# The sample's cached attention in a hybrid encoder step: one group of tokens, or shared between two

## The chip, the core and the metric

The kernel runs on one core of one Trainium2 chip. Its time is the device time of one execution in microseconds (us). A core has five engines, each with an in-order queue: TensorE (PE; its weight loads are listed as PEld), VectorE (DVE), ScalarE (ACT), GpSimd (POOL) and SyncE (SP), which here only issues DMA transfers. Matrix products land in eight PSUM banks of 128 x 512 fp32 numbers; everything else lies in SBUF or in main memory.

## The reference

One layer with two branches of 8 heads of 128 channels each, over 1024 new frames of a prompt (eight tiles of 128 rows) and 8 x 16 frames of running streams (one tile, the sample), with cached keys and values of 1024 past frames for each stream:

```python
h = rms_norm(x, norm_pre)                       # x: (rows, 2048)
p = h @ w_in                                    # 8 column blocks of 1024:
q_sb, k_sb, v_sb, gate_sb, q_r, k_r, v_r, gate_r = split(p)
# stick-breaking branch, strictly causal; of the sample over cache and new keys
z = q_sb @ k_sb.T * 128 ** -0.5
log_keep = where(strict, log_sigmoid(-z), 0)
a = where(strict, exp(log_sigmoid(z) + later(log_keep)), 0)
o_sb = a @ v_sb
# retention branch: rope on q_r, k_r, decay masks, running state in and out
y = concat(head_rms_norm(o_sb) * silu(gate_sb), head_rms_norm(o_r) * silu(gate_r))
x + rms_norm(y @ w_out, norm_post)
```

The new keys, values and states are outputs too.

## The kernel before

The rows are worked in two groups: the first is tiles 0 to 3 and the sample (640 columns of the transposed activations, in pieces of 256 and 384), the second tiles 4 to 7 (512 columns, one piece). Each group runs through the eight heads. For a head, `project` makes the columns 4, 5 and 7 of the input projection (retention's query, key, gate), then 0, 1 and 3 (the stick-breaking query, key, gate); `project_rows` makes the value rows of both heads of a pair at the even head. Weights and activations are split in a high and a low part, and each product is made of three (`products`, line 206, 48 steps for a projection). This is most of PE's work; its weights come through SP's queue in small loads (L192, L237) that ACT and DVE split (L127, L128).

Everything else is done by jobs: generators that are advanced by `tick()`, one job at most for each step of `products`, and that say after how many ticks they want the next turn. The constants `D_...` hold these waits; where one is a pair, the first is for the first group. They decide where in PE's program a job's matmuls stand. The engines' queues are then filled by a list scheduler when the kernel is built, and the hardware runs each queue in order.

For each head there is a job for retention (`ret_branch`), one for the prompt's attention (`sb_branch`, with `stick_breaking`: scores z at L535, the value product at L559), and in the first group one for the sample (`decode`), which lasts about one head's period:

- Keys: sixteen chunks of cached keys, each by four DMAs of POOL's queue (L585, buffer kc), are transposed by DVE (L610, kcT). After four chunks, four matmuls of 32 rows, one for each column tile, make a quarter of the scores (zc, L601); two quarters share one PSUM bank of the pool psz, which has three. ACT takes two sigmoids of each half (kp at L459, be at L460). The scores against the new keys (zn, L626) go into another bank of psz.
- Weights: `weights` masks on POOL, then DVE scans (L476) and multiplies (L477). `turn_out` writes the result to a scratch tile s_bd through ACT's queue, `turn_in` reads it back in four pieces through SP's (L441), and DVE transposes it into kp (L635).
- Values: the new values (L641), then eight sets of four 32-row matmuls over the cached values (L648, buffer vc), accumulate in a bank of psa, the pool with one bank that the prompt's and retention's products use too. The cached values come in eight loads of 512 KB through SP's queue (L616). They share five buffers (`V_BUFS`) with kcT; five loads are put in the queue at once, ahead of the scores' end.

The normalisation and gate of the sample's result are done with the prompt's, in one `Out` of five tiles. Beside it, the sample's retention state is worked in `retention` (pSs, L739), in both versions in the first group.

Between the groups `load_moving` brings the second group's activations (s_h, staged in the first 50 us) through four buffers mr of SBUF and splits them, tied to the last gate's and the next query's projection; the same function brings the gated results s_y to the output projection. The first output panel (`panel0`, L889 to L891) is made beside the last jobs.

## Time and profile before

| | before |
|---|---|
| time, median of 3 runs | 2466.65 us |
| lowest and highest | 2466.45, 2468.67 us |
| profiled execution: span | 2465.5 us |
| matmuls on PE | 14832 |
| moved by DMA | 418.65 MB, mean 170 GB/s |

The span lies 1.15 us under the median; what the time has beyond the span lies around the first and last instruction. From the trace's timeline the execution has these stages, in us from the span's start: normalising and staging the rows, 0 to 50; the first group, to 1172; the second, to 2027; the last jobs beside the first output panel, to 2082; the output projection, to 2465. In the views, a matmul's row gives its line, its tiles (out<-in), its shape, and how many equal ones follow each other; "idle before" is what the engine waited just ahead of it, and for whom.

### The profile page before, as it was taken

To read this page: it belongs to the slowest core of one execution; us is meant where nothing else is said; L and a number is where in the kernel's file an instruction comes from. 1 tells how busy PE (TensorE), PEld (TensorE's weight loads), DVE (VectorE), ACT (ScalarE), POOL (GpSimd) and SP (SyncE) were. 2 spreads that over 40 slices of the span, in tenths; PEclk is the share of its full clock that TensorE was granted. 3 is DMA by queue.
4 is the path that set the end of the run, shared out by engine and by line. 5 is a ranking of instruction groups with operands and counts; after the bars stand their busy time and mean duration, and the time that the engine had idled before them with its cause. 6 is when DMAs were issued, how large, how long until landed. Compare 5 with 4: busy or idle time off the path is not lost.

```text
span 2465.5 us, 40324 instructions
## 1 busy us (share of the span) xinstructions
PE 2368.1 (96%) x14832; PEld 2098.0 (85%) x14832; DVE 1250.1 (51%) x2362; ACT 904.3 (37%) x1913; POOL 643.7 (26%) x1029
## 2 busy tenths in 40 slices
PE   7999899989999999999899999999999998999998
PEld 7999889879898888989588898888889877778787
DVE  8245454444444454445545554554564565564544
ACT  6323232323223232323334434344344343543343
POOL 3244353433344344333402111120220211000000
PEclk9999999999999999999899999999999999999999
DMA  7769788785958768598955665565664566765554
GB/s 242 167 151 208 145 199 165 173 171 138 210 134 202 160 155 189 134 217 177 219 153 149 155 152 145 143 164 134 154 158 128 153 151 179 242 215 163 184 182 135
DMA packets 673094, 418.65 MB, mean 170 GB/s; under 512 B 223744, under 2 KB 617984, under 8 KB 670464
## 3 DMA queue, kind: packets, MB, share of 16 engines
q1 hardware_dynamic: 523760, 285.99, 46.3%
q0 software_dynamic: 32256, 71.36, 12.9%
q10 hardware_dynamic: 116880, 58.74, 8.5%
q8 instruction: 116, 1.90, 0.3%
q14 instruction: 82, 0.67, 0.1%
HBM read 336.24 MB, written 79.69 MB: 169 GB/s over the span
## 4 chain that ended last, share of the span: by engine, by line
PE 72%; DMA 12%; issue 8%; DVE 5%; ACT 1%; POOL 1%; SPq 1%; DVEq 0%; ACTq 0%; POOLq 0%
PE acc L206 37%; PE accn L252 14%; PE a L890 4%; PE a L891 4%; PE a L889 4%; PE pa L559 2%; DMA vc<-cache_sb_v 2%; PE z L535 1%; DMA s_be<-kb 1%; DMA wr<-w_in 1%; DMA mr<-s_y 1%; PE zc L601 1%; DMA kb<-s_be 1%; DMA kc<-cache_sb_k 1%; DMA ro<-s_rk 1%
## 5 line engine op out<-in xcount | busy, mean ns | idle before, releaser
L206 PE MATMUL acc<-mh,wh 128*128 128x256 f32 (+2 forms) x2304 | 670.8, 341 | 6.8 <-ACT rv L262 4.3
L206 PE MATMUL acc<-ml,wh 128*128 128x256 f32 (+2 forms) x2304 | 676.5, 343 | 0.0
L206 PE MATMUL acc<-mh,wl 128*128 128x256 f32 (+2 forms) x2304 | 670.3, 341 | 6.1 <-DVE wl L128 6.1
L128 DVE TENSOR_TENSOR wl<-wr,wh 128x512 fp32r<-128x512 f32 (+1 forms) x576 | 395.2, 690 | 531.9 <-ACT wh L127 522.0
L127 ACT ACTIVATE wh<-wr 128x512 fp32r<-128x512 f32 (+1 forms) x576 | 357.6, 625 | 756.6 <-PE acc L206 366.5
L206 PEld LDWEIGHTS acc<-mh,wh 128*128 128x128 f32 x2304 | 425.6, 189 | 51.5 <-issue 14.5
L206 PEld LDWEIGHTS acc<-mh,wl 128*128 128x128 f32 x2304 | 425.0, 189 | 50.4 <-issue 12.4
L206 PEld LDWEIGHTS acc<-ml,wh 128*128 128x128 f32 x2304 | 422.5, 189 | 39.5 <-issue 12.4
L585 POOL DMA_DIRECT2D kc<-cache_sb_k x512 | 331.4, 653 | 374.9 <-DVE kcT L610 175.0
L252 PE MATMUL accn<-whn,mh 128*128 128x256 f32 x1152 | 332.8, 290 | 1.1 <-ACT whn L127 1.1
L252 PE MATMUL accn<-wln,mh 128*128 128x256 f32 x1152 | 327.1, 284 | 5.6 <-DVE wln L128 5.6
L252 PE MATMUL accn<-whn,ml 128*128 128x256 f32 x1152 | 326.8, 284 | 0.0
L252 PEld LDWEIGHTS accn<-whn,mh 128*128 128x128 f32 x1152 | 221.5, 192 | 14.6 <-issue 11.0
L252 PEld LDWEIGHTS accn<-wln,mh 128*128 128x128 f32 x1152 | 221.7, 192 | 8.6 <-DVE wln L128 7.2
L890 PE MATMUL a<-wl,mh 128*128 128x512 f32 (+1 forms) x576 | 220.7, 383 | 7.8 <-DVE wl L128 7.7
L252 PEld LDWEIGHTS accn<-whn,ml 128*128 128x128 f32 x1152 | 221.4, 192 | 1.7 <-issue 1.7
L889 PE MATMUL a<-wh,mh 128*128 128x512 f32 (+1 forms) x576 | 219.2, 383 | 3.6 <-ACT wh L127 2.6
L891 PE MATMUL a<-wh,ml 128*128 128x512 f32 (+1 forms) x576 | 220.3, 382 | 0.0
L890 PEld LDWEIGHTS a<-wl,mh 128*128 128x128 f32 x576 | 108.7, 189 | 31.2 <-DVE wl L128 10.6
L127 ACT ACTIVATE whn<-wrn 128x512 fp32r<-128x512 f32 x128 | 79.8, 634 | 151.2 <-PE acc L206 38.3
L889 PEld LDWEIGHTS a<-wh,mh 128*128 128x128 f32 x576 | 109.0, 189 | 26.4 <-ACT wh L127 4.1
L441 POOL DMA_DIRECT2D be<-s_be x128 | 94.0, 741 | 139.8 <-DMA s_be<-be 122.3
(184 smaller groups left out, 2578.8 us busy)
## 6 DMA issues: line engine op xcount, KB each, us to landing
wr<-w_in SPq DMA_DIRECT2D x384, 256.0 KB, 4.0
wr<-w_out SPq DMA_DIRECT2D x184, 256.0 KB, 3.5
wrn<-w_in SPq DMA_DIRECT2D x128, 256.0 KB, 3.3
kc<-cache_sb_k POOLq DMA_DIRECT2D x512, 64.0 KB, 4.5
vc<-cache_sb_v SPq DMA_DIRECT2D x64, 512.0 KB, 8.5
xt<-x_prompt SPq DMA_DIRECT2D x8, 1024.0 KB, 6.5
xr<-x_prompt SPq DMA_DIRECT2D x8, 1024.0 KB, 6.6
out<-out ACTq DMA_DIRECT2D x12, 512.0 KB, 2.9
```

Source lines behind the costliest of these rows:

```text
L127: nc.scalar.activation(hi, src, AF.Copy)
L128: nc.vector.tensor_tensor(lo, src, hi.bitcast(F32), ALU.subtract)
L206: last = nc.tensor.matmul(a[:, :m], lhs[:, j, :], rhs[w][:, j, o : o + m], start=(w == 0 and j == 0 and n == 0), stop=(w == KT // WQ - 1 a ...
L252: nc.tensor.matmul(a, lhs[q][:, jj, ts], rhs[:, j, :], start=(w == 0 and j == 0 and n == 0 and t % 2 == 0), stop=(w == KT // 2 - 1 and j = ...
L441: q.dma_start(raw[32 * i : 32 * i + 32, :].rearrange("p (k a) -> p k a", a=32), s[:, :, 32 * i : 32 * i + 32].rearrange("k (j b) a -> b (k ...
L535: nc.tensor.matmul(z[:, :c], q2[a][:, i * P : (i + 1) * P], k2[b][:, s : s + c], start=(m == 0), stop=(m == 2),)
L559: nc.tensor.matmul(po[:, :P], at[:, j, :], vn[:, j, :], start=(j == 0), stop=(j == t))
L585: nc.gpsimd.dma_start(kc[32 * i : 32 * i + 32, :].rearrange("p (k d) -> p k d", d=32), cache_k[0, 2 * c + j, s * 512 : (s + 1) * 512, h, 3 ...
L601: nc.tensor.matmul(z[r, :], qp[:, j, r], ready[c // 2][:, c % 2, :], start=(j == 0), stop=(j == 1))
L889: nc.tensor.matmul(a[:, :width], hi[q][:, j, ts], wh, start=(k == 0), stop=False)
L890: nc.tensor.matmul(a[:, :width], hi[q][:, j, ts], wl, start=False, stop=False)
L891: nc.tensor.matmul(a[:, :width], lo[q][:, j, ts], wh, start=False, stop=(k == KT - 1))
```

## The change

The sample's stick-breaking heads are shared between the groups: the even heads' query, key and gate are made in the first group, the odd ones' in the second, which takes the heads of a pair in the other order (1, 0, 3, 2, and so on). A group's heads without the sample have 512 columns in one piece, those with it 640 in two. A decode job runs over two head periods, with larger waits, in a bank of its own (psd; psz goes from three banks to two), with an `Out` and an end of its own (`ends`, scratch s_ys). The four score matmuls of a quarter are kept together, tile 3 first. Cached values are loaded one by one, and the buffers shrink: three for kcT and vc, two for kc, two for mr. The scores of five tiles come in 512 + 128 columns (computed as 256) where they were 384 + 256, as old and new keys now lie in two tiles of 512. s_h holds the sample's rows too.

```diff
-D_ZC = 12
-D_ROW = 18
-D_VC = 9
-V_BUFS = 5
+D_ZC = 24
+D_ROW = 24
+D_VC = 20
+D_DTO = 40
+D_DTI = 20
+D_DTR = 6
+V_BUFS = 3
...
+    def takes_sample(gi, h):
+        return h % 2 == gi
...
-            r = wp.tile([P, n], F32, name="mr", tag="mr", bufs=4)
-            nc.sync.dma_start(r, src(k))
+            r = wp.tile([P, n], F32, name="mr", tag="mr", bufs=2)
+            for o, m, ap in src(k):
+                nc.sync.dma_start(r[:, o : o + m], ap)
...
+                    nc.vector.tensor_tensor(
+                        hs[:, WQ * q : WQ * (q + 1), :],
+                        mov[0][q][:, :, NB_TOK:].bitcast(F32),
+                        mov[1][q][:, :, NB_TOK:].bitcast(F32),
+                        ALU.add,
+                    )
...
-        psz = s1.enter_context(tc.tile_pool(name="psz", bufs=3, space=PSUM))
+        psz = s1.enter_context(tc.tile_pool(name="psz", bufs=2, space=PSUM))
         psa = s1.enter_context(tc.tile_pool(name="psa", bufs=1, space=PSUM))
+        psd = s1.enter_context(tc.tile_pool(name="psd", bufs=1, space=PSUM))
...
         def z_pieces(n):
-            if n == 5 * P:
-                return (0, 3 * P), (3 * P, 2 * P)
             return [(s, min(512, n - s)) for s in range(0, n, 512)]
...
-        def decode(h, out, qs, rest):
+        def decode(h, qs, rest):
+            out = Out(1, "os")
...
-                kc = ip.tile([P, 512], F32, name="kc", tag="kc", bufs=3)
+                kc = dp.tile([P, 512], F32, name="kc", tag="kc", bufs=2)
...
-                    for c in range(4):
+                    done = None
+                    for c in (3, 0, 1, 2):
                         r = slice(32 * c, 32 * c + 32)
-                        nc.tensor.matmul(
+                        with tc.issue_after(done.ins) if done else nullcontext():
+                            mm = nc.tensor.matmul(
...
-            values = [load_v(k) for k in range(V_BUFS)]
-            while "kT" not in rest:
+            while "ks" not in rest:
                 yield 3
-            z = psz.tile([P, 512], F32, name="zn", tag="z")
+            z = bank("zn")
...
             turned = turn_out(be.rearrange("p (k c) -> p k c", c=P), f"s_bd{h}")
-            yield D_TO[phase[0]]
+            load_v()
+            yield D_DTO
             turn_in(turned, be, nc.sync)
-            yield D_TI[phase[0]]
+            load_v()
+            yield D_DTI
             nc.vector.transpose(kp[:, :n], be)
-            yield D_TR[phase[0]]
+            load_v()
+            yield D_DTR
...
-            po = acc_tile()
+            po = bank("pd")
...
-                if k + V_BUFS < 8:
-                    values.append(load_v(k + V_BUFS))
+                if len(values) < 8:
+                    load_v()
...
         for gi, g in enumerate(GROUPS):
...
+            for i in range(H):
+                h = i ^ gi
+                sample = takes_sample(gi, h)
+                pieces = WITH_SAMPLE if sample else PROMPT_ONLY
...
-                acc = project(g, mov, col(0, h))
+                acc = project(pieces, mov, col(0, h))
...
+                if sample:
+                    drain(dec_job)
+                    while len(ends) > 1:
+                        drain(ends.pop(0))
...
+                    dec_job = Job(decode(h, qs, rest), D_DEC)
```

How this moves the instructions is seen in the engines' programs, where each row is a line, an operation and its tiles, with a count of equal ones in a row. First PE at the end of a head's cache scores; this is the last head of the first group before:

```order
L601 MATMUL zc<-kcT,qp 32x512 x2
L626 MATMUL zn<-kT,qs 128x128
L559 MATMUL pa<-vn,kb 128x128
L601 MATMUL zc<-kcT,qp 32x512
L535 MATMUL z<-kh,qh 128x512
L535 MATMUL z<-kl,qh 128x512
L535 MATMUL z<-kh,ql 128x512
L206 MATMUL acc_13148<-mh_12926,wh 128x512
L206 MATMUL acc_13148<-ml_12927,wh 128x512
L252 MATMUL accn_13294<-whn,mh_12778 128x256
```

And PE at the last decode that begins in the first group now (L622 is the cache score's line, L650 the new key's, L216 the projection's):

```order
L622 MATMUL zc<-kcT,qp 32x512 x4
L216 MATMUL acc_11342<-mh_159,wh 128x512
L216 MATMUL acc_11342<-ml_160,wh 128x512
L216 MATMUL acc_11342<-mh_159,wl 128x512
L216 MATMUL acc_11342<-mh_159,wh 128x512
L729 MATMUL pS<-rv,rkn 128x128
L216 MATMUL acc_11342<-ml_160,wh 128x512
L650 MATMUL zn<-ks,qs 128x128
L216 MATMUL acc_11342<-mh_159,wl 128x512
```

The set of four stood in three places, with zn ahead of some of them; now it is one piece, and zn follows it.

Second, SP's queue at one head's value loads (L616 before) and the return of the turned weights (be); wr, wrn are weights, st and dT belong to retention:

```order
L616 DMA vc<-cache_sb_v 128x8x128 x4
L192 DMA wr<-w_in 128x4x128 x4
L724 DMA st<-state_ret 128x2x128
L192 DMA wr<-w_in 128x4x128 x2
L616 DMA vc<-cache_sb_v 128x8x128
L192 DMA wr<-w_in 128x4x128
L441 DMA be<-s_bd_5630 32x36x32 x4
L192 DMA wr<-w_in 128x4x128 x4
L616 DMA vc<-cache_sb_v 128x8x128 x3
```

The same queue now (L642 is the value load, L459 the return, L202 the weights):

```order
L642 DMA vc<-cache_sb_v 128x8x128
L459 DMA so<-s_o_2_4_5508 32x16x32 x4
L459 DMA ro<-s_rk_3_5670 32x20x32 x4
L202 DMA wr<-w_in 128x4x128 x8
L642 DMA vc<-cache_sb_v 128x8x128 x2
L202 DMA wr<-w_in 128x4x128 x2
L459 DMA be<-s_bd_5861 32x36x32 x4
L202 DMA wr<-w_in 128x4x128 x4
L691 DMA dT<-c_dt 128x256
```

Of the five value loads ahead of the return three are left; the other five follow one by one behind the value products.

Third, PE beside the first output panel (a), where a decode now has its value products (L667 and L674, bank pd):

```order
L576 MATMUL pa<-vn,kp 128x128 x5
L667 MATMUL pd<-vs,kp 128x128
L674 MATMUL pd<-vc,kp 32x256 x12
L961 MATMUL a_21334<-wh_21675,mh_21301 128x512
L961 MATMUL a_21335<-wh_21675,mh_21301 128x512
L961 MATMUL a_21336<-wh_21675,mh_21301 128x512
L962 MATMUL a_21334<-wl_21676,mh_21301 128x512
L963 MATMUL a_21334<-wh_21675,ml_21302 128x512
L962 MATMUL a_21335<-wl_21676,mh_21301 128x512
L963 MATMUL a_21335<-wh_21675,ml_21302 128x512
L962 MATMUL a_21336<-wl_21676,mh_21301 128x512
L674 MATMUL pd<-vc,kp 32x256 x4
```

Before, only the prompt's value products (pa<-vn,kp) stood among these panel matmuls; now three sets of the decode's stand in one piece behind them, and the fourth eight panel matmuls later.

236 lines of the change are left out of this document (141 added, 95 removed).

## The prediction

> **What bounds the kernel now.** I read the page's busy line first, then its chain that ended last, then the busy time by stage, then PE's waits stage by stage.
>
> ```profile
> PE 2368.1 (96%) x14832; PEld 2098.0 (85%) x14832; DVE 1250.1 (51%) x2362; ACT 904.3 (37%) x1913; POOL 643.7 (26%) x1029
> PE 72%; DMA 12%; issue 8%; DVE 5%; ACT 1%; POOL 1%; SPq 1%; DVEq 0%; ACTq 0%; POOLq 0%
> ...
> 50.00:338.00 288.00, 280.01 (x2038) 262.20 (x2037) 131.17 (x267) 95.06 (x203) 106.97 (x176) 0.99 0.75 166
> 1390.00:1596.00 206.00, 205.73 (x1178) 180.70 (x1177) 109.61 (x192) 82.97 (x171) 36.07 (x56) 1.00 0.59 149
> 2027.00:2082.00 55.00, 44.97 (x203) 36.18 (x202) 33.43 (x50) 22.14 (x47) 15.91 (x23) 0.94 0.80 207
> ```
>
> The first line is the page's, the next the shares of the chain, the rest stretches of the span with the busy time of PE, PEld, DVE, ACT and POOL, the granted clock, the DMA share and GB/s. PE is the bound: 96% busy, 72% of the chain. A pair of heads in the first group, whose work runs from 50 to 1172, takes 288 us and leaves PE idle for 8 of them, with DMA at 0.75. The second group, from 1172 to 2027, has no decode beyond its first 60 us; a pair there takes 206.00 us, of which PE is busy 205.73, with DMA at 0.59. So the decode's waits can only be won in the first group, and the second is a place without slack into which half of the decode moves.
>
> PE's waits (engine, line, released by: us in all, times, longest), four lines of the first group, then two of the stretch from 2027 on:
>
> ```profile
> PE pa L648 <- DMA vc<-cache_sb_v: 9.3, 4, 4.6
> PE pa L641 <- DVE kp L635: 8.0, 2, 7.3
> PE pa L559 <- DVE so L656: 7.5, 3, 4.0
> PE zc L601 <- DVE kcT L610: 3.5, 3, 2.1
> ...
> PE a L890 <- DVE wl L128: 7.7, 5, 3.0
> PE pa L559 <- DVE kp L525: 6.7, 3, 2.9
> ```
>
> The four are all the decode's: its cached values late, its turned weights late, the prompt's value products kept out of the one shared bank until the decode's result is read, its transposed keys late. Together 9.3 + 8.0 + 7.5 + 3.5 = 28.3 us, the most that removing them can save directly.
>
> **The change part by part.** Terms are against the profiled execution, whose span is 2465.5 us; the shown median, 2466.65, lies 1.15 above it, and I add the sum to the median.
>
> (a) **Matmul pieces.** PE pays for each switch to the decode's 32-row matmuls:
>
> ```profile
> 1197.11 1.05 PE L601 MATMUL zc<-kcT,qp 128*32 128x512 f32 x4
> 1198.10 0.49 PE L626 MATMUL zn<-kT,qs 128*128 128x128 f32 x2
> ...
> 1199.52 1.04 PE L601 MATMUL zc<-kcT,qp 128*32 128x512 f32 x2 [0.71 <-DVE kcT L610]
> 1200.50 0.50 PE L535 MATMUL z<-kh,qh 128*128 128x512 f32 x1
> ...
> 661.14 0.64 PE L648 MATMUL pa<-vc,kp 128*32 128x256 f32 x8
> 661.71 0.38 PE L252 MATMUL accn<-whn,ml 128*128 128x256 f32 x1
> ...
> 172.99 0.71 PE L739 MATMUL pSs<-rv,rkn 32*128 32x128 f32 x8
> ...
> L535 PE MATMUL z<-kl,qh 128*128 128x512 f32 x40 | 15.8, 395 | 0.0
> L535 PE MATMUL z<-kl,qh 128*128 128x384 f32 x24 | 8.1, 338 | 0.0
> ```
>
> From a start to the next, a piece of cache scores (zc) takes 0.99 us with 4 records and 0.98 with 2: splitting a set of four column tiles costs the whole piece again. In PE's program the pieces fall from 45 to 32, since the four are now held together: 13 x 0.98, **-13 us**. The pieces of the value product over the cache rise from 55 to 63, at 661.71 - 661.14 = 0.57 us: +4.6. Those of the sample's retention state (pSs) rise from 16 to 23; between nothing and 0.71 each I take 0.3, as most of such a piece is its own work: +2. Of the 384-column scores of the prompt 24 become 512 wide: 24 x (395 - 338) ns = +1.4. Together **+8 us**. All main matmuls keep their counts; the sample columns merely move between the groups.
>
> (b) **The four waits of the first group.** A head has twice the time, the bank is the decode's own, and half the heads are gone. The shared-bank wait (7.5) goes; of the others I leave 4 us: **-24 us** (bounds 0 and -28.3). What is late next there is the turn of (d).
>
> A long wait also costs clock (columns as in the stretches above):
>
> ```profile
> 520.00:525.00 5.00, 0.00 (x0) 0.00 (x0) 0.80 (x2) 1.26 (x2) 0.67 (x2) 0.70 1.23 203
> 525.00:530.00 5.00, 3.68 (x22) 2.22 (x23) 4.44 (x9) 0.97 (x2) 0.00 (x0) 0.50 0.14 24
> 530.00:535.00 5.00, 5.00 (x32) 4.40 (x31) 1.12 (x2) 0.63 (x1) 0.00 (x0) 0.77 0.65 170
> ```
>
> After the 7.3-us wait the clock is 0.50, and 0.77 in the next stretch: with PE busy 3.68 at half rate and 5.00 at 0.77, some 1.8 + 1.2 = 3 us are lost, 0.4 per us waited. For the waits of 7.3, 4.6 and 4.0: **-6 us**. [...]
>
> (c) **The new bank.** Cache scores and new-key scores (zn) now take turns in one bank, so zn waits for the sigmoids of the second half of the cache scores:
>
> ```profile
> L459 ACT ACTIVATE kp<-zc x16: 578/598/602, 167.2 to 1208.6; 128x512 f32<-128x512 f32 x16
> 1405.98 23.83 PE acc L206 x104
> ```
>
> The first row is one of two such sigmoids, together 1.2 us after the scores; the second is a stretch of the chain in the second group, 23.83 / 104 = 0.229 us a main matmul. zn stands about six of those behind the scores, 1.4 us. The cover is just enough if ACT comes at once; behind zn stands the whole projection. I take 8 x 0.4 = 3 us, and 2 for prompt scores with two banks instead of three: **+5 us** (bounds 0, and 20 if ACT, 37% busy, is mostly occupied).
>
> (d) **The turn of the decode's weights** (scan, product, out to memory, back, 32x32 transpose), between zn and the first value product:
>
> ```profile
> 630.02 0.49 PE L626 MATMUL zn<-kT,qs 128*128 128x128 f32 x2
> 636.80 2.56 DVE L476 TENSOR_TENSOR_SCAN kp<-kp 128x1152 f32<-128x1152 f32 x1 [1.04 <-ACT kp L459]
> 639.49 1.36 DVE L477 TENSOR_TENSOR be<-be,kp 128x1152 f32<-128x1152 f32 x1
> 651.20 3.59 SPq L441 DMA_DIRECT2D be<-s_bd  x4
> 659.22 1.38 DVE L635 STREAM_TRANSPOSE kp<-be 128x1152 f32<-128x1152 f32 x1 [5.49 <-DMA be<-s_bd]
> 660.75 0.46 PE L641 MATMUL pa<-vn,kp 128*128 128x128 f32 x2
> ...
> s_bd<-be ACTq DMA_DIRECT2D x8, 576.0 KB, 7.9
> be<-s_bd SPq DMA_DIRECT2D x32, 144.0 KB, 4.8
> ...
> DMA to landing us min/median/max: 2.3/5.1/10.3
> ```
>
> Here the chain took 660.75 - 630.02 = 30.7 us, of which 659.22 - 640.85 = 18.4 was the way through memory and 12.3 the rest. With both ways at 2.3, the shortest landing (the last row is of the scratch tile), and 3.6 for issuing the four returns, the way is 8.2 and the chain 20.5; with the medians, 7.9 and 4.8, it is 28.6. In PE's program of the new kernel 72 main matmuls at 0.229 (16.5 us), 17 of the prompt's scores and five of its value products (4.1) stand between the two in the second group, 20.6 us; in the first about five more, and for the very last decode 58 main matmuls (13.3) and 5.3 of scores, 18.6. In the first group it is covered. In the second the DMA share was 0.59 and rises to about 0.68 with the caches; I take the middle, 24.5: a stall of 3.9 us in three decodes, 11 to 12, and, these being short, 1 to 2 for the clock: **+13 us** (bounds 0 and +45). Behind the waiting product stand all projections.
>
> (e) **From group to group** the moving rows are staged again, now through two buffers instead of four, and 640 wide instead of 512, while a decode runs its value product:
>
> ```profile
> 1210.00:1220.00 10.00, 7.37 (x56) 7.04 (x54) 9.01 (x12) 1.59 (x4) 4.09 (x5) 0.92 1.00 283
> 1220.00:1230.00 10.00, 4.54 (x19) 4.04 (x19) 2.75 (x6) 1.89 (x3) 3.68 (x6) 0.50 0.91 219
> ```
>
> Before, this place already lost 2.6 + 5.5 = 8 us idle and about 2.3 to the clock, with DMA full. The last decode of the first group again stands here, and in PE's program its first twelve value matmuls (three loads) are in one piece; the fourth load can begin only when the first has been used. **+3 us** (bounds -10, all of it gone, and +15).
>
> (f) **The tail.** One decode now ends beside the first output panel, where before there was none:
>
> ```profile
> vc<-cache_sb_v SPq DMA_DIRECT2D x64, 512.0 KB, 8.5
> ```
>
> Again three loads are used in one piece, the fourth lands 8.5 us later, with some 2 us of panel matmuls ahead of it in the queue: 6.5, and the turn has 18.6 of cover for 24.5: 5.9. Part coincides with the 6.7 us that PE waits there for the prompt's turned weights: 12.4 less about half of that, **+9 us** (bounds -3 and +20).
>
> (g) **At no cost:** staging the sample's rows (four more DVE sums and one write, in the start, beside projections); the issues of cached keys, with two buffers for three, since a chunk has at least 24 products x 0.229 = 5.5 us, two 11, for four issues of 0.649, a landing of 4.5 and a transpose; V loads one by one, each behind its buffer in SP's queue, with the weights' loads behind them:
>
> ```profile
> L585 POOL DMA_DIRECT2D kc<-cache_sb_k x512: 649/649/871, 105.4 to 1202.2; - x171
> kc<-cache_sb_k POOLq DMA_DIRECT2D x512, 64.0 KB, 4.5
> ```
>
> If those covers fail, each head pays a wait like the 4.6 above.
>
> **Sum:** -13 + 8 - 24 - 6 + 5 + 13 + 3 + 9 = -5; 2466.65 - 5 = 2461.65, given as **2462 us**.
>
> **The rivals.** A: the turn fits its cover also in the second group and the tail costs little. Then (d) is 0, (e) 0, (c) +3, (f) +3: -13 + 8 - 24 - 6 + 3 + 3 = -29, **2438**. For it speaks the lower DMA share of the second group; against it that even the shortest chain, 20.5, has 0.1 us to spare.
>
> B, on the other side: the chain keeps its 30.7 us in the second group, because DVE's in-order queue and SP's, not DMA, make it. Three decodes stall 30.7 - 20.6 = 10.1 us, 30, and 0.4 x 30 = 12 for the clock: +42 for +13, **2491**. The stall, with its clock, costs 3 x 1.4 us per us of chain; all else makes -18, so it decides against the change from 20.6 + 18 / 4.2, about 25 us, and by a measurable amount from 26. For it speaks the 10.3 us from the product's end, 640.85, to the return's issue, 651.20; against it that this was at DMA 0.74 and over.
>
> C: two staging buffers starve the change of groups; at +18 instead of +3, +15, and the fourth V load at the same place, a little: **2478**.
>
> [...]
>
> **How the numbers follow.** A measurement of this kernel can tell about 0.2%, 4.9 us, so faster is below 2461.7 and slower above 2471.6. The forecast, with its own range 2450 to 2474, has 0.42 (0.20 faster, 0.17 same, 0.05 slower); A 0.26, B 0.23, C 0.07, D 0.02. Faster 0.46, same 0.17, slower 0.37. The range runs from 2430, A with the transition's idle time gone too, to 2490, nearly B: half of B lies beyond it, D, and a little of A.
>
> **What would show it.** In the new profile: zc in pieces of full sets, 32 of them; no wait of the prompt's value product for the decode's result; waits for cached values under 4 us in the first group. The wait of the new-value product (pd from the turned kp) is the decisive line: 0 in the second group for A, about 3 x 4 for the forecast, 3 x 10 at a clock of 0.5 for B. A pair there should take 206 us, plus 4 x 0.98 and 8 x 0.57 for the decode's pieces and, for the sample's columns of one head, a quarter of 144 x 0.229, some 223, plus these stalls; a wait of zn for ACT of over a microsecond would show (c) too small. I am wrong altogether if the second group waits on its weights, since I priced SP's queue at nothing.

## The result

The changed kernel takes 2523.27 us (median of 4, 2519.45 to 2527.46) against 2467.66 us for the kernel before on the same chip: ratio 1.0232, 95% interval 1.0213 to 1.0251. It is slower by 2.3%, some 56 us, where 2462 us and a range up to 2490 were forecast.

The page of the changed kernel, its busy line:

```profile
PE 2388.8 (95%) x14832; PEld 2111.3 (84%) x14832; DVE 1271.1 (50%) x2454; ACT 908.0 (36%) x1939; POOL 643.6 (26%) x1029
```

The span of this execution is 2517.7 us, 52.2 more than before's 2465.5. PE is busy 2388.8 - 2368.1 = 20.7 us longer and idle 31.5 us longer. The longer busy time goes with a lower clock: the matmuls are the same in number, and the mean granted clock is 0.975 where it was 0.987. Where the time is lost is seen when the span is cut at the first projection of the second group and at the first matmul of the output panel. First the kernel before, then the changed one (stretch, its length, busy time of PE, PEld, DVE, ACT, POOL, granted clock, DMA share, GB/s):

```profile
50.00:1172.00 1122.00, 1082.71 (x7871) 996.47 (x7870) 528.93 (x1068) 349.96 (x775) 434.53 (x722) 0.99 0.76 171
1172.00:2022.00 850.00, 836.90 (x4778) 723.55 (x4777) 449.29 (x800) 336.32 (x696) 154.67 (x244) 0.99 0.61 153
2022.00:2465.00 443.00, 414.05 (x1947) 344.45 (x1945) 233.50 (x400) 183.47 (x390) 34.50 (x33) 0.98 0.60 187
```

```profile
50.00:1064.00 1014.00, 992.24 (x6923) 924.35 (x6923) 475.05 (x1003) 337.00 (x737) 282.73 (x481) 0.99 0.65 154
1064.00:2052.00 988.00, 937.63 (x5663) 804.52 (x5662) 520.42 (x944) 354.51 (x754) 306.63 (x484) 0.97 0.74 166
2052.00:2517.00 465.00, 424.32 (x2010) 348.80 (x2009) 237.34 (x411) 182.24 (x395) 34.25 (x35) 0.96 0.61 189
```

Idle time of PE is length less busy. In the first group it falls from 39.3 to 21.8 us (-17.5), in the second it rises from 13.1 to 50.4 (+37.3), from the first panel on from 29.0 to 40.7 (+11.7). The first group ends 108 us earlier, as it should with half the decode gone, and the second lasts 138 us longer.

PE's waits in the changed kernel (engine, line, released by: us in all, times, longest):

```profile
PE z L552 <- ACT be L479: 24.5, 8, 6.7
PE accn L262 <- DVE rk L305: 18.0, 3, 6.5
PE pa L576 <- DVE kp L541: 16.4, 5, 8.3
...
PE pd L674 <- DMA vc<-cache_sb_v: 9.2, 6, 3.2
PE acc L216 <- ACT mh L136: 8.3, 4, 4.2
...
PE zc L622 <- DVE kcT L632: 5.2, 4, 1.3
...
PE pd L667 <- DVE kp L661: 1.8, 2, 1.0
```

The decode's own waits are nearly gone: 1.8 us for its turned weights (before 8.0), none of the prompt's value products for the decode's result (7.5). But the three largest are new or grown, and none of them is the decode's: the prompt's scores wait for a sigmoid, the value rows for the rotary sums of the keys, the prompt's value product for its turned weights.

### The wait for the sigmoid

ACT in the second group, at the end of a decode's scores (start, us, engine, line; ACTq rows are issues of DMA in ACT's queue), then PE and DVE at the same place:

```profile
1321.28 0.62 ACT L478 ACTIVATE kp<-z 128x512 f32<-128x512 f32 x1
1321.64 0.40 ACTq L810 DMA_DIRECT2D out<-kn  x1
1328.38 0.39 ACTq L453 DMA_DIRECT2D s_bd<-be  x1
1331.98 0.32 ACTq L810 DMA_DIRECT2D out<-kn  x1
1332.48 0.60 ACT L479 ACTIVATE be<-z 128x512 f32<-128x512 f32 x1 [10.59 <-DMA vc<-cache_sb_v]
```

```profile
1326.03 0.39 PE L216 MATMUL acc<-mh,wl 128*128 128x512 f32 x1
1333.13 0.80 PE L552 MATMUL z<-kph,qh 128*128 128x512 f32 x1 [6.72 <-ACT be L479]
1333.72 0.63 PE L552 MATMUL z<-kpl,qh 128*128 128x512 f32 x1
```

```profile
1325.12 1.32 DVE L496 TENSOR_TENSOR be<-be,kp 128x1152 f32<-128x1152 f32 x1
```

The prompt's scores z need two sigmoids before their bank is free. The first (kp) is done at 1321.90. Between it and the second (be) ACT's program has the write of the decode's turned weights, which needs DVE's product, ready at 1326.44, and a key output. Neither takes ACT half a microsecond by itself; but the queue is in order, and the write goes out at 1328.38, the key output at 1331.98. ACT stands 10.59 us, PE 6.72, and after it PE's matmuls take 0.63 us where they took 0.39: the clock has fallen (0.50 from 1333 to 1338 us). It comes back at the next decodes: PE waits 5.96 and 5.05 us there, and 2.99 and 1.86 at the last.

That the key output waits from 1328.8 to 1331.98 is for a transfer and not for ACT: the profile puts ACT's idle time, 10.59 us, on the landing of a value load of SP's queue. Two of these loads were issued there, at 1320.47 and 1320.96. The first took 7.8 us to land, to about 1328.3, and the write goes out at 1328.38, 1.94 us after DVE's product; the second landed at 1331.96, and the key output goes out 0.02 us later. The chain that ended last has this second load (start, us, what):

```profile
1320.96 0.03 SPq L642
1320.99 0.03 issue
1321.02 10.95 DMA vc<-cache_sb_v
1331.96 0.02 issue
1331.98 0.32 ACTq L810
```

Neither issue uses the loaded values; why they go out only at these landings the trace doesn't show.

### The wait for the rotary sums

In the first group, at the start of every second head from the third on (POOL, DVE and PE of the changed kernel):

```profile
571.02 0.77 POOL L453 DMA_DIRECT2D s_be<-kb  x1 [8.50 <-DVE kb L496]
577.07 2.47 POOL L459 DMA_DIRECT2D kb<-s_be  x4 [5.28 <-DMA s_be<-kb]
```

```profile
584.39 0.58 DVE L541 STREAM_TRANSPOSE kb<-kb 128x384 f32<-128x384 f32 x1 [5.45 <-DMA kb<-s_be]
```

```profile
588.28 0.55 PE L262 MATMUL accn<-whn,mh 128*128 128x256 f32 x1 [6.25 <-DVE rk L305]
```

The prompt's weights of a tile go out at 571.02 and are back at 584.39, 13.4 us later. DVE's program has their transpose too early, DVE stands 5.45 us at it, and the keys' rotary sums, queued behind, hold the banks that the value rows need. Before, the same tile of the fourth head had from 634.9 to 652.2, 17.3 us, and no wait. The way itself is no slower: the median landing of the return fell from 5.8 to 4.1 us (48 KB pieces). What shrank is the time that the order leaves for it. The waits of the jobs are counted in ticks, one for a step of a projection, and in the first group's heads without the sample a step is now one matmul of 512 columns, 0.229 us, and not the pair of 0.147 each, 0.294 (18.48 us for 126 matmuls in the kernel before's chain of waits). So the 33 ticks of `D_TB`, which are a part of that time, are 7.6 us where they were 9.7.

### The profile page after: what moved, and what is told of

Read it like the earlier page. It is cut to its first block, busy times and chain, and to the rows that moved or that the text cites. A ratio compares the mean times of both kernels' runs of the same rounds, so it can differ in the third digit from the quotient of the medians.

```text
span 2517.7 us, 40551 instructions
## 1 busy us (share of the span) xinstructions
PE 2388.8 (95%) x14832; PEld 2111.3 (84%) x14832; DVE 1271.1 (50%) x2454; ACT 908.0 (36%) x1939; POOL 643.6 (26%) x1029
## 4 chain that ended last, share of the span: by engine, by line
PE 76%; DMA 11%; issue 6%; DVE 4%; POOL 1%; ACT 1%; SPq 0%; DVEq 0%; ACTq 0%; POOLq 0%
PE acc L216 41%; PE accn L262 15%; PE a L962 3%; PE a L963 3%; PE a L961 3%; DMA mr<-s_y 2%; PE pa L576 2%; DMA s_be<-be 2%; PE z L552 1%; DMA vc<-cache_sb_v 1%; DMA mr<-s_h 1%; PE zc L622 1%; DMA s_be<-kb 1%; DMA kb<-s_be 1%; POOL be L459 1%
## 5 line engine op out<-in xcount | busy, mean ns | idle before, releaser
L216 PE MATMUL acc<-mh,wh 128*128 128x512 f32 (+2 forms) x2304 | 665.1, 342 | 9.3 <-ACT mh L136 8.3
L216 PE MATMUL acc<-mh,wl 128*128 128x512 f32 (+2 forms) x2304 | 666.2, 342 | 4.5 <-DVE wl L137 4.5
L216 PE MATMUL acc<-ml,wh 128*128 128x512 f32 (+2 forms) x2304 | 667.5, 343 | 0.1
L216 PEld LDWEIGHTS acc<-mh,wh 128*128 128x128 f32 x2304 | 424.3, 189 | 56.1 <-issue 15.0
L216 PEld LDWEIGHTS acc<-mh,wl 128*128 128x128 f32 x2304 | 425.3, 189 | 41.1 <-DVE wl L137 7.6
L216 PEld LDWEIGHTS acc<-ml,wh 128*128 128x128 f32 x2304 | 424.7, 190 | 37.2 <-issue 7.5
L137 DVE TENSOR_TENSOR wln<-wrn,whn 128x512 fp32r<-128x512 f32 x128 | 88.8, 701 | 111.1 <-ACT whn L136 111.1
```

Source lines behind the costliest of these rows:

```text
L137: nc.vector.tensor_tensor(lo, src, hi.bitcast(F32), ALU.subtract)
L216: last = nc.tensor.matmul(a[:, :m], lhs[:, j, :], rhs[w][:, j, o : o + m], start=(w == 0 and j == 0 and n == 0), stop=(w == KT // WQ - 1 a ...
```

## The experiments

All ratios are to the kernel before, run beside each version on the same chip, with 95% intervals; the changed kernel has 1.0232 [1.0213, 1.0251]. One caution holds for all: an edit moves the whole program of every engine, since a list scheduler orders it, so a time alone proves little. The wait that was to go is read each time, and below, behind e14, where in the execution the time changed.

### Each suspected wait alone

**e1**, the write later:

```diff
-D_ROW = 24
+D_ROW = 40
```

> Edit: the decode's wait ahead of its turn, D_ROW, is 40 ticks and not 24, so that in ACT's program the write of the turned weights (s_bd) stands behind the sigmoids of the prompt's first scores. Queue theory (ACT's in-order queue holds the s_bd issue, which waits for DVE's product, and a key output behind it, which waits for an earlier transfer, ahead of the second sigmoid of the prompt's scores; PE then stands at the next scores because the bank is not read): PE's wait of z for ACT's be falls from 24.5 us to under 5, and the time from 2523 to 2495-2503. Bank theory (two banks for scores are too few however ACT is ordered): the wait stays over 15 us and the time within 6 us of 2523. Third possibility: the later write makes the turned weights late and the wait moves to the new-value product (pd), over 10 us.

Measured: 2507.82 us, 1.0180 [1.0152, 1.0208]. In the waits of e1:

```profile
PE pd L674 <- DMA vc<-cache_sb_v: 18.3, 7, 6.0
PE acc L216 <- ACT wh L136: 12.6, 3, 6.2
...
PE accn L262 <- DVE rk L305: 10.0, 3, 3.5
PE pd L667 <- DVE kp L473: 8.7, 3, 2.9
...
PE z L552 <- ACT be L479: 5.3, 2, 3.3
```

The wait for the sigmoid falls from 24.5 to 5.3 us: the write's place in ACT's queue makes that wait, as the queue theory has it. The time falls by 13 to 15 us and not by 20 to 28. The write, later in ACT's queue, now holds the split of the next weights (wh 12.6), the cached values come later, and PE waits for the decode's turned weights: 2.9 us at each of three decodes of the second group, 8.7 in all (the line named as releaser, L473, is a small fill right behind their transpose in DVE's queue). The wait for the rotary sums, which the edit does not aim at, falls from 18.0 to 10.0 us. So the gain needn't be that of the sigmoid, and by stage, below, it isn't.

**e2**, the same write from another queue:

```diff
-            turned = turn_out(be.rearrange("p (k c) -> p k c", c=P), f"s_bd{h}")
+            turned = turn_out(be.rearrange("p (k c) -> p k c", c=P), f"s_bd{h}", nc.gpsimd)
```

> Edit: the s_bd write is issued from POOL's queue and not from ACT's; nothing else. Queue theory: as in e1, the wait of z for ACT falls, to under 8 us since the key outputs stay in ACT's queue and POOL now holds the prompt's selects for 2 to 4 us; time 2497-2510. Bank theory: no change, 2517-2529.

Measured: 2525.88 us, 1.0246 [1.0217, 1.0276]. The wait falls to 15.4 us in 8, longest 3.8, so both expectations of the wait miss; the time is the bank theory's. The key outputs still stand in ACT's queue ahead of the sigmoid, and nothing is gained: the waits for cached values (13.0), wh (11.8) and wl (10.5) take its place.

**e3**, more ticks in the first group:

```diff
-D_TB = (33, 33)
+D_TB = (42, 33)
```

> Edit: D_TB, the wait between a prompt tile's weights and their turn, is 42 ticks in the first group and not 33. Tick theory (a tick is one step of a projection, 0.23 us in a head without the sample's columns and 0.29 with them, so the same 33 ticks are now 7.5 us where they were 9.6; the prompt's turned weights then come after their place in DVE's in-order queue, which holds the rotary sums of the keys, for which PE waits): the wait of the value rows for rk (18.0 us, three times about 6) falls below 4, and the time from 2523 to 2496-2507. Rival (the way through memory itself became slower by the new traffic): the wait stays over 12 us, the time within 6 us of 2523.

Measured: 2504.16 us, 1.0161 [1.0129, 1.0193]. The wait for rk falls from 18.0 to 5.5 us, and the time by 17 to 19. By the wait alone this isn't decided, since in e2 (above) and e4 (below), with the ticks of the changed kernel, it falls as well, to 4.0 and 4.3 us. What decides is DVE's stand at the transposes of the prompt's turned weights, in the changed kernel and in e3:

```profile
DVE kb L541 <- DMA kb<-s_be: 94.9, 21, 14.2
```

```profile
DVE kb L541 <- DMA kb<-s_be: 57.3, 22, 6.0
```

In e2 it is 105.2 us and in e4 98.6, in the kernel before 59.9. In e2 and e4 PE waits at the same place for another product of DVE, the split of the next weights (wl: 3.34 us at 579.55 in e2, 4.18 at 573.38 in e4); with more ticks DVE itself stands less. And e3's gain lies in the first group, as the table below shows. The rival, a slower way through memory, would have kept the stand.

**e4**, the decode's own bank undone (its scores in the prompt's pool, three banks; its value products in the shared one):

```diff
-        psz = s1.enter_context(tc.tile_pool(name="psz", bufs=2, space=PSUM))
+        psz = s1.enter_context(tc.tile_pool(name="psz", bufs=3, space=PSUM))
...
-                return psd.tile([P, 512], F32, name=name, tag="pd")
+                if name == "pd":
+                    return acc_tile()
+                return psz.tile([P, 512], F32, name=name, tag="z")
```

> Edit: the decode's own PSUM bank is undone: its scores go into the prompt's pool, which has three banks again, its value products into the bank that all value products share. Bank theory: the wait of z for ACT is under 3 us and the time 2495-2503. Queue theory: a third bank takes up one more piece of scores, 2 to 3 us of each of the 6-us waits, so 8 to 14 us of wait stay; the prompt's value products wait again for the decode's result, 4 to 8 us; time 2508-2525.

Measured: 2526.87 us, 1.0255 [1.0222, 1.0288]. The wait of z for be falls to 2.2 us, as the bank theory had it and more than the queue theory granted: a third bank covers ACT's stand. But the turned weights (14.9), the cached values (15.9) and the next weights (13.4) wait in its place. So the bank is the place where ACT's stand becomes PE's; giving it back doesn't give back the time.

**e5**, e1 and e3 together (`D_ROW` 40, `D_TB` 42 in the first group):

> Edit: D_ROW 40 (as in e1) and D_TB 42 in the first group (as in e3) together. If the two waits have causes of their own (ACT's queue in the second group, ticks in the first), the gains add: 2523 - 15 - 19, 2485-2494. If a removed wait only moves to the next late thing, less than two thirds of that: over 2500.

Measured: 2486.96 us, 1.0089 [1.0059, 1.0119]. The gains add: 35 to 36 us of the 56. That they come from the two places that the expectation names is shown for the ticks only (table below).

### What is left in ACT's queue

In e5 ACT still stands at the write, now ahead of the gate's sigmoid and the split of the next weights (ACT of e5):

```profile
1528.86 0.27 ACT L479 ACTIVATE be<-z 128x128 f32<-128x128 f32 x1
1534.36 0.39 ACTq L453 DMA_DIRECT2D s_bd<-be  x1
1535.87 0.36 ACTq L526 DMA_DIRECT2D s_y<-rg  x1
1536.28 0.60 ACT L289 ACTIVATE sg<-acc 128x512 f32<-128x512 f32 x1 [7.14 <-DMA wr<-w_in]
```

**e12**, e5 with the write from POOL's queue (the edit of e2):

> Edit on e5: the s_bd write from POOL's queue. In e5 ACT's queue still stands some 5 us at that write, now ahead of the gate's sigmoid and the split of the next weights (PE's waits for wh, 10.6 us). If that is a cost of its own: the wait for wh falls below 4 and the time to 2473-2481. If POOL's selects behind the write take its place, as in e2: within 5 us of 2487.

Measured: 2478.32 us, 1.0061 [1.0040, 1.0083]; wh falls from 10.6 to 5.8 us, not below 4. Some 7 to 9 us less than e5, with intervals that still overlap, though the same edit gave nothing in e2; the wait of z for ACT is 10.4 us, in e5 7.9. What still holds ACT is seen in its program at the same place (ACT of e12):

```profile
1288.38 0.62 ACT L478 ACTIVATE kp<-z 128x512 f32<-128x512 f32 x1
1288.64 6.13 ACTq L810 DMA_DIRECT2D out<-kn  x2
1294.97 0.60 ACT L479 ACTIVATE be<-z 128x512 f32<-128x512 f32 x1 [5.97 <-DMA out<-kn]
```

Two issues of key outputs stretch over 6.13 us, again between the two sigmoids.

**e13** and **e14**, e12 with the key outputs from SP's or POOL's queue (here e14; the sample's outputs alike, and `nc.sync` in e13):

```diff
-                nc.scalar.dma_start(
+                nc.gpsimd.dma_start(
                     k_prompt[0, 0, tiles[0] * P : (tiles[0] + 4) * P, h, ds].rearrange("(j b) a -> b j a", b=32),
...
```

> Edit on e12 (2478): the new keys' outputs are issued from SP's queue and not from ACT's. In e12 ACT still stands 6.1 us at such an issue (2 of them, beginning at 1288.64 us), ahead of the sigmoid that frees a bank of scores. If that is the rest of the second group's loss: the wait of z for ACT (10.4 us) falls below 4 and the time to 2464-2472. If the issue only holds SP instead, and with it the weights: PE waits for wl or wh over 10 us and the time is 2475 or more.

> Edit on e12: the new keys' outputs are issued from POOL's queue. Same theory as e13: wait of z for ACT below 4. POOL pays 4 issues of some 0.65 us a head (8 with the sample's) and its selects may come late: 2464-2480; over 2480 if POOL becomes the one that is waited for.

Measured: by SP 2537.92 us, 1.0274 [1.0242, 1.0305]; by POOL 2465.61 us, 0.9988 [0.9970, 1.0006]. Waits of e13, then of e14:

```profile
PE pa L576 <- DVE kp L541: 35.7, 5, 10.8
...
PE z L552 <- ACT be L479: 2.0, 3, 0.7
```

```profile
PE pa L576 <- DVE kp L541: 13.3, 6, 2.8
...
PE z L552 <- ACT be L479: 7.8, 3, 7.1
```

From SP, the queue of the weights and of the returns, the wait of z goes, but the time is worse by 60 us than in e12, the prompt's turned weights come late, and PE waits 14.5 and 11.5 us for weights (wl, wh), as the second expectation had it. From POOL the time is that of the kernel before: with four repairs (`D_ROW`, `D_TB`, and the two kinds of write out of ACT's queue) the sharing costs nothing, and gains nothing. Of the wait for z, e14 keeps one of 7.1 us, so my expectation of under 4 missed there; ACT stands 6.17 us there for the landing of an earlier write of a gate (s_y<-sg: three such waits in e14, 14.6 us together).

Where the time changed can be read from the place of zn, which each decode has once: from the first decode's to the fourth's lie three pairs of heads of the first group, from the fourth's to the fifth's the change of groups, from the fifth's to the eighth's three pairs of the second group. Lengths in us, one profiled execution each, with the starts of zn:

| | first group | change of groups | second group | rest, to the end of the span |
|---|---|---|---|---|
| changed kernel | 782.9 (260.49 to 1043.38) | 276.7 (to 1320.05) | 726.8 (to 2046.82) | 470.9 (to 2517.7) |
| e1 | 772.9 (261.58 to 1034.46) | 269.7 (to 1304.20) | 734.7 (to 2038.92) | 471.9 (to 2510.8) |
| e3 | 762.8 (261.83 to 1024.61) | 275.1 (to 1299.71) | 734.0 (to 2033.75) | 471.9 (to 2505.6) |
| e4 | 780.8 (259.07 to 1039.89) | 256.4 (to 1296.30) | 740.8 (to 2037.11) | 487.8 (to 2524.9) |
| e5 | 757.0 (260.07 to 1017.10) | 264.7 (to 1281.82) | 729.4 (to 2011.23) | 481.4 (to 2492.6) |
| e12 | 759.8 (260.07 to 1019.82) | 267.3 (to 1287.16) | 718.2 (to 2005.38) | 470.5 (to 2475.9) |
| e14 | 760.9 (263.84 to 1024.71) | 267.8 (to 1292.48) | 712.0 (to 2004.46) | 464.0 (to 2468.5) |

e3, whose edit leaves the second group's ticks alone, differs by 7 us there, so a difference of that size says little. Two things stand out. The ticks are worth 20 us in the first group, where the tick theory puts them, and e5, e12 and e14 keep that gain. But in e1, e4 and e5, where most of z's wait is gone, the second group is no shorter than in the changed kernel: what PE no longer waits for at z it waits for elsewhere. It gets shorter only with the issues out of ACT's queue, by 9 us in e12 and 15 in e14. So the queue makes the wait of 24.5 us, but its price in the second group, as far as these runs tell, is about 15 us; and e1's gain lies in the first group and the change of groups, for a reason that no run isolates.

### Parts of the change alone

**e6**, the sharing alone undone: all decode in the first group, one head period each with the old waits, the smaller buffers and the own bank kept.

```diff
-        return h % 2 == gi
+        return gi == 0
...
-D_ZC = 24
-D_ROW = 24
-D_VC = 20
-D_DTO = 40
-D_DTI = 20
-D_DTR = 6
+D_ZC = 12
+D_ROW = 18
+D_VC = 9
+D_DTO = 26
+D_DTI = 12
+D_DTR = 3
...
```

> Edit: the sharing alone is undone: all heads' decode, with its projections' sample columns, in the first group, over one head period each with the old waits (12, 18, 9, 26, 12, 3); the own bank, the smaller buffers, the single loads, the kept-together scores and the own end of the decode stay. Sharing theory (the loss comes from the second group and the tail, where the decode's issues and transposes get into queues that have no slack, and from shorter ticks in the first): the second group is without waits of z for ACT, the tail as before, and the time 2450-2475. Resources theory (two banks for scores, three value buffers, two staging buffers make the loss wherever the decode runs): 2495 or more, with the waits for cached values back over 10 us in the first group.

Measured: 2574.00 us, 1.0435 [1.0398, 1.0473], 51 us slower than with sharing: the opposite of the sharing theory. PE's first waits in e6:

```profile
PE pa L576 <- DVE kb L541: 41.3, 13, 5.9
PE pd L674 <- DMA vc<-cache_sb_v: 35.6, 22, 2.9
```

The resources theory holds. With the change's small buffers and banks, a head's period is too short; two periods save 51 us of that.

**e7**, the kept-together scores alone, in the kernel before (the same lines as in the change):

> Kernel before with one part of the change alone: the four matmuls of a set of cache scores are kept together, tile 3 first. 45 pieces become 32, 0.98 us each: the time falls by 10 to 14 us, to 2452-2457, if PE pays for each piece; if the pieces were hidden in waits anyway, it stays within 4 us of before.

Measured: 2478.77 us, 1.0051 [1.0031, 1.0070]: slower by 11 us, where a gain of 12 was expected. PE does work less on the scores, but waits:

```profile
PE pa L559 <- DVE so L659: 12.8, 5, 3.9
PE zc L603 <- DVE kcT L613: 11.5, 4, 6.7
```

The wait for transposed keys was 3.5 to 4.2 us. A set that was split let PE use the early chunks; kept together, with tile 3 first, it stands until the last has come, and all behind it, too.

**e8**, two staging buffers (`mr`) alone, in the kernel before:

> Kernel before with one part of the change alone: two buffers for the staged rows (mr) and not four. If these starve the change of groups and the loads for the output panel, each of the two places loses 4 to 10 us: 2475-2486. If staging is bound by DMA there anyway: within 4 us of before.

Measured: 2467.68 us, 1.0006 [0.9986, 1.0026]: nothing.

**e10**, the smaller rings alone, in the kernel before:

```diff
-V_BUFS = 5
+V_BUFS = 3
...
-                kc = ip.tile([P, 512], F32, name="kc", tag="kc", bufs=3)
+                kc = ip.tile([P, 512], F32, name="kc", tag="kc", bufs=2)
```

> Kernel before with two parts of the change alone: three buffers for turned keys and cached values, not five, and two for key chunks, not three; banks and sharing as before. Resources theory, buffers: with one head's period the loads then come late, the waits for cached values and turned keys grow from 13 us to 40 or more and the time to 2510-2560, as in e6. If the bank is what made e6 slow: within 10 us of before.

Measured: 2507.84 us, 1.0174 [1.0145, 1.0204], just under the range of the resources theory, with its waits. The waits of e10, and the group of its score matmuls with busy time and mean, which was 47.6 us in the kernel before:

```profile
PE pa L648 <- DMA vc<-cache_sb_v: 44.2, 22, 3.4
```

```profile
L601 PE MATMUL zc<-kcT,qp 128*32 128x512 f32 x256 | 70.5, 605 | 9.4 <-DVE kcT L610 9.2
```

**e11**, the own bank alone, in the kernel before (psz two banks, zc, zn and the value product in psd):

> Kernel before with one part alone: the decode's scores and value products have a bank of their own, and the prompt's scores two banks and not three. Bank theory of e6: the time rises by 20 us or more, with waits of z or pS for ACT or DVE. If the bank is a gain (the 7.5 us that the prompt's value product waits for the decode's result go, and little comes): 2455-2464.

Measured: 2499.30 us, 1.0144 [1.0121, 1.0167]:

```profile
PE zn L627 <- ACT be L461: 14.0, 5, 4.0
```

Here zn does wait for the sigmoids of its shared bank, 14 us, and not z, as I had written. The four parts alone, +11, 0, +44 (2507.84 - 2463.54) and +36 (2499.30 - 2463.54), sum to 91 us; e6, which has them all and besides the single loads and the decode's own end, loses 106.

### Three that went wrong

**e9**, the last decode of each group faster, on e5:

```diff
+            d_zc, d_vc = (18, 12) if last else (D_ZC, D_VC)
...
```

> Edit on e5 (2487): the last decode of each group has 18 ticks for a chunk of keys and 12 for a set of values, the others keep 24 and 20, so that less of it stands at the change of groups and beside the first output panel. If what is left of the loss, 19-20 us, lies mostly in the decode's value product at those two places (20 us of waits for cached values in e5), the wait for values falls below 10 and the time to 2468-2478. If the key loads and not the ticks set the pace, the program hardly changes and the time stays within 5 us of 2487.

Measured: 2499.05 us, 1.0142 [1.0116, 1.0167]. The wait for values did fall, from 20.0 to 5.6 us, but the staged rows (mh 12.0) and the prompt's turned weights (14.7) are waited for instead: 12 us slower than e5. What the work at the change of groups and beside the panel costs by itself is not settled by it.

**e15**, the queues of e14 in the kernel before (the write and the key outputs from POOL):

> Kernel before with the two issues moved that the changed kernel was mended by: the write of the turned weights and the key outputs from POOL's queue. If they hold ACT as much there, before gains 10 us or more as well (2450-2457) and sharing still loses against it; if three banks of scores and PE's place for them covered them, the time stays within 6 us of 2467, or grows since POOL issues every head's keys within one period.

Measured: 2523.18 us, 1.0229 [1.0192, 1.0267]; cached values are waited for 30.2 us, before 9.3, and the prompt's turned weights 21.9, before 6.7. The repair belongs to the changed kernel; in the kernel before, with every head's decode in one period, it is a loss.

**e16**, still more ticks, on e14 (`D_TB` 46 and 42):

> Edit on e14 (2465.6): D_TB 46 in the first group and 42 in the second, not 42 and 33, since PE still waits 13.3 us for the prompt's turned weights (kp). If their chain is just too short of ticks there too, as in e3: that wait below 5 and 2452-2460. If the later turn is only waited for later (the end of a head, the tail): 2462-2475.

Measured: 2511.64 us, 1.0190 [1.0143, 1.0236]. The wait for turned weights falls only from 13.3 to 9.5 us, and z waits 21.9 for the split of the keys (kh) on ACT. So a few ticks alone moved the time by 46 us, nearly as much as the repairs together: gains and losses of this size hang on where the order happens to put things. No run was faster than the kernel before by more than its interval. More ticks (`D_TB`, `D_ROW`) in the kernel before were not tried, so whether that kernel would gain by them too is open.

## Why the prediction was wrong

The **sum** was -5 us and the measured difference +56. By its own steps, from the profiles (it is added up rightly; what failed are its terms):

(a) The pieces: **half right**. The groups of the changed kernel, with busy time and mean (those of before: zc 47.6, the cached value product 41.3, pSs 11.9 us):

```profile
L674 PE MATMUL pd<-vc,kp 128*32 128x256 f32 x512 | 49.9, 444 | 9.2 <-DMA vc<-cache_sb_v 9.2
L622 PE MATMUL zc<-kcT,qp 128*32 128x512 f32 x256 | 34.1, 605 | 5.2 <-DVE kcT L632 5.2
L767 PE MATMUL pSs<-rv,rkn 32*128 32x128 f32 x128 | 16.5, 296 | 0.0
```

Scores fall by 13.5 us, -13 forecast. The value products rise by 8.6 (4.6), pSs by 4.6 (2 forecast; over seven more pieces that is 0.66 each, so a split piece seems to cost it all again, as zc did). So these three come to near nothing and not to -5; and e7 shows that the saving on the scores is not the kernel's, since it is paid back in waits when it stands alone.

(b) The four waits: **right**, and what comes late next: **wrong**. The decode's waits left the first group. But the -6 us for the clock had the wrong sign: with new long waits the mean clock fell to 0.975, and PE was busy 20.7 us longer. The step that failed is "What is late next there is the turn of (d)": it was the prompt's own turned weights, 18.0 us, since the ticks of half the heads got shorter. The order listing showed these heads with one piece of 512; I priced them as work moved and not as a clock of the jobs. e3 shows it: 17 to 19 us of the time, in the profiled execution 20 us of the first group.

(c) The new bank: "2 for prompt scores with two banks instead of three" **failed**, and with it the place of the risk. z waited 24.5 us. The prediction gave no row for the 2 (with three banks the wait was 0.2 us) and took its bound from ACT's busy share, 37%, where ACT was not busy but standing, 10.59 us, at two DMA issues. Even the bound of 20 was too small, the clock after the waits not counted. The trace and e1 show ACT's queue as the cause of the wait, e4 the bank as the place; what it costs is seen in e12 and e14, 9 to 15 us of the second group. zn, for which I took 3, is not among the waits; it is in e11, at 14.0.

(d) The turn: it cost nothing in the second group, by luck. From zn at 1320.05 to the first value product of the same head:

```profile
1353.35 0.38 PE L667 MATMUL pd<-vs,kp 128*128 128x128 f32 x2
```

That is 33.3 us, against the 20.6 of cover that I had counted. The chain itself is at most 32.6 (its transpose on DVE ends at 1352.60), and PE didn't wait for it: the stand of PE at z, 6.72 us, and the slower clock after it lengthened the cover. The 1.8 us of PE's waits for it fall at the change of groups and beside the panel. With z's stand gone, in e1 and e5, the stall that (d) forecast is there, 2.9 us at each of three decodes (3.9 forecast), though there DVE is busy right up to the transpose, so its queue and not the way through memory comes last. That short stalls cost the clock only the 1 to 2 us of (d), no run shows: at the 0.4 us per us waited of (b), 11 to 12 us would cost 4 to 5, and after a wait of 2.50 us in the changed kernel the clock was 0.53 (last section). So +13 did not come, and the time went past B's 2491 by another mechanism than B's.

(e) The change of groups: +3 forecast. The stretch in the kernel before, then in the changed one:

```profile
1172.00:1235.00 63.00, 50.72 (x269) 38.03 (x268) 35.81 (x65) 23.09 (x47) 28.00 (x46) 0.89 0.93 220
```

```profile
1064.00:1130.00 66.00, 48.56 (x223) 30.49 (x222) 31.57 (x66) 21.80 (x42) 21.59 (x36) 0.77 0.84 206
```

PE idles 17.4 us and not 12.3, about 5 more. The clock is 0.77 and not 0.89, which by my estimate, 0.12 of the 48.56 busy us, is 6 more: some 11 us, within the bounds of -10 and +15. Rival C's cause, two staging buffers, is excluded for the kernel before by e8; for the changed one, with rows 640 wide and 8.3 us of waits for the staged rows (mh), it stays open, since more buffers weren't tried there.

(f) The tail: +9 forecast, +11.7 idle: the number **right**, its making not, so partly luck. Of the two waits of the decode that I had added to 12.4 us, 4.8 came (3.9 for values, 0.9 for the turn); the prompt's turned weights took 13.4 us there, before 6.7, and z's sigmoid 4.9.

(g) At no cost: POOL's issues kept their median of 649 ns with DVE 50% busy, and no run shows DVE holding them up, which was rival D with its 0.02. No cached values were waited for in the first group, since two periods cover the small rings; with one period, in the kernel before, those rings cost 44 us (e10). The single value loads are not free, though: at 1328 and 1332 us they are what the issues in ACT's queue waited for.

The signs that I had named told little. The line that I called decisive, PE's wait for the turned weights at the second group's decodes, came out at 0, as for A, with the time beyond B; zn didn't wait for ACT, and PE waited only 3.5 us for weights (wl, wh, wln, whn) between 1064 and 2052 us. Only the pair's length showed the loss: some 223 us plus stalls forecast, 240.2 to 245.7 measured from zn to zn.

So the range failed at two places that the prediction did not have: an in-order queue in which DMA issues stand ahead of what frees a bank, and a clock of ticks that ran faster. With the ticks and the write mended 42 to 45 us of the 56 are gone (e12), and with the key outputs all of it (e14). By stage the ticks are about 20 us of that and the queue about 15; the rest, at the change of groups and in the tail, is not attributed, and e15 and e16 are the caution. Seen the other way round, e6 says that the change without the sharing loses 106 us, and that the sharing wins back 51.

## What to carry to other kernels

An engine that is 37% busy can still be what PE waits for at one place (ACT in the changed kernel, 36% busy there: 24.5 us of PE's waits): read its queue for DMA issues that wait, between a bank's last matmul and the instruction that frees it, before taking a bank away. Where waits are written as counts of steps, a change of a step's size retunes every job that counts them (33 ticks, 9.7 us before and 7.6 after). And a count of pieces saved is not time saved unless the operands of the whole piece are there: the early pieces were doing work in time that is idle otherwise (e7: 11.5 us of waits for turned keys, before 3.5 to 4.2). Last, a wait that is gone from the list is not time gained: read beside it whether the stage got shorter (e1: 24.5 us of waits down to 5.3, the second group 734.7 us where it was 726.8).

## What the runs showed of the hardware

The issue of a DMA can hold its engine: in the changed kernel the median issue of a key output takes 0.44 us of ACT's queue, but in e12 two of them stretched over 6.13 us, with a wait in between, and the sigmoid behind them came 5.97 us late. And a wait of PE costs more than its length: after 6.72 us a matmul took 0.63 us and not 0.39, at a granted clock of 0.50 from 1333 to 1338 us, so three waits of 5 to 7 us in the second group are among what takes its granted clock from 0.99 to 0.97.

A shorter wait cost clock as well. PE in e1, after 3.22 us:

```profile
324.75 0.36 PE L262 MATMUL accn<-whn,mh 128*128 128x256 f32 x1 [3.22 <-DVE rk L305]
...
326.64 0.42 PE L262 MATMUL accn<-wln,mh 128*128 128x256 f32 x1
```

In the rows right behind the first such a matmul took 0.28 us, two microseconds later 0.42; the granted clock from 324.8 to 328 us is 0.66. In the changed kernel, after PE's wait of 2.50 us that ended at 1406.96, it is 0.53 from 1407 to 1410 us. So waits of 2.5 to 3.2 us were not free of the extra price here.
